# SiLU of the gates placed behind the last softmax exponential in a hybrid attention and recurrence layer

## The chip, the cores and the metric

The kernel runs on one core of one Trainium2 chip. The metric is the device time of one execution in microseconds (us), lower being better. The core has five engines with a program each: PE (TensorE, matrix products; its weight loads are listed as PEld), DVE (VectorE), ACT (ScalarE), POOL (GpSimd) and SP (SyncE, which here only starts transfers). Each engine executes its own program strictly in order; they wait for each other by semaphores. All numbers are float32, and each product is made of three passes over high and low halves (fp32r).

## The reference, cut to what matters

One encoder layer on 512 tokens of width 2048. A single input projection gives six parts:

```python
h = rms_norm(x, norm_w)
q, k, v, g_attn, xr, g_lru = split(h @ w_in)
attn_out = attention_group(q, k, v, ...)        # 8 heads of 128, 2 key/value heads, softmax over 512 keys
lru_out  = lru_group(xr, ...)                   # convolution, gated linear recurrence in both directions
mixed = concat([rms_norm(attn_out) * silu(g_attn), rms_norm(lru_out) * silu(g_lru)])
return x + mixed @ w_out
```

The part that matters here is `silu(g_lru)` and the first quarter of `silu(g_attn)`, and when they are computed relative to the softmax.

## The kernel before, in words

The layer is written as stages along PE's time. First the projection of `xr` and the recurrence, then k, v and q, then, from about 256 to 434 us of the profile, the attention. The attention's products leave PE with gaps while softmax runs elsewhere, so a second stream of work is woven into it: `fill = gates()`, a generator. The attention yields small numbers of steps, and `weave(fill, attention(rots))` takes so many steps of `gates()` between its pieces. A step `n` of `gates()` is half a letter of `PLAN`: `u` is a block of the recurrence's gate `g_lru` (`gl_units`, seven products P1, Q6, P2, Q5, Q3, Q7, Q4 of a Strassen-Winograd scheme, whose sums end in eight tiles `halves_of`, named ev in the profile), `G` a block of the first 256 columns of `g_attn` (`ga_units`, two tiles `early`), `H` a block of the next 256 columns (`late`).

Beside each step a side generator `todo` may take a step: the gating. `lru_gates(j)` handles four ev tiles, tokens by features: SiLU with the scale `rstd` (L1228), a second scaling by `r_lru` (L1231), and four groups of four transposes on PE (L1236) into one PSUM bank each, from which DVE multiplies into `hp`, the recurrence's output (L1240). `heads_gates` applies SiLU to the two `early` tiles (L1248) and multiplies into the first heads on DVE (L1252). In the kernel before, `lru_gates(0)` and `heads_gates` are started when the last `G` is done and `lru_gates(1)` when Q4 is done.

Softmax is in `softmax`: the row maximum on DVE (L626), its scaling on ACT (L627), the exponential on ACT (L630), a reciprocal on DVE and the division on POOL (L632). It is done 32 times (8 heads, 4 blocks of queries). The weights are transposed on PE (L639) and split on ACT and DVE (L581, L582). `values` multiplies them with v and copies the result on ACT (L652).

ACT also makes the high half of each weight tile (`wsplit`, L224, tiles wr to wh; for `ga_units` L1211) and of the second operand of the scheme (draw to dh, L1183); DVE makes the low halves (wl, L226 and L1212; dl, L1184). wr has three buffers, and wh and wl four each.

What orders an engine's program: PE, POOL and (in this stage) the transfers follow the order of the code; for ACT and DVE a scheduler chooses by priorities and by when inputs are ready. `tc.issue_after(ins)` adds an order on one engine: what is recorded inside stands behind `ins` in that engine's program. It adds no semaphore.

Exponential and SiLU need different function tables on ACT. Between them stands an instruction ACT_TABLE_LOAD, put there by the compiler wherever the function changes from one table to the other; copies and Identity need no change.

Of the kernel before, what the change touches and what calls it, by code (L numbers as in the profile page):

```python
# [13 lines left out]
AF = mybir.ActivationFunctionType  # L14
# [11 lines left out]
G = NH // NKV  # L26
# [36 lines left out]
def hybrid_kernel(  # L63
# [20 lines left out]
    nc = tc.nc  # L84
# [30 lines left out]
    def nm(s):  # L115
        cnt[0] += 1
        return f"{s}_{cnt[0]}"
# [7 lines left out]
    def k2(dt=F32, shape=(P, SEQ)):  # L125
        pool, n, _ = work()
        return pools[pool].tile(list(shape), dt, tag="k2", bufs=n, name=nm("k2"))
# [11 lines left out]
    def pj():  # L139
        return ps.tile([P, SEQ], F32, tag="pj", name=nm("pj"))  # L140

    def mm():
        return ps.tile([P, SEQ], F32, tag="mm", name=nm("mm"))

    def const(shape, name, dt=F32):
        return cp.tile(list(shape), dt, tag=name, name=name)
# [45 lines left out]
    def v1(r):  # L192
        return vec[:, r : r + 1]
# [95 lines left out]
    rstd = const([P, NT], "rstd")  # L289
# [320 lines left out]
    def weights(q, g, t, r, by):  # L610

        qh, ql = q
        tt = slice(t * P, (t + 1) * P)
        sc = mm()
        mm3(sc, qh[:, tt], ql[:, tt], kth[g], ktl[g], True, True)
        return soon(softmax, sc, r, by=by)

    def soon(what, *given, by=SOON):

        with tc.high_priority(by):  # L620
            return what(*given)

    def softmax(sc, r):

        mx = pools["att"].tile([P, 1], F32, tag="mx", bufs=16, name=nm("mx"))
        nc.vector.tensor_reduce(mx, sc, axis=AX.X, op=ALU.max, negate=True)  # L626
        nc.scalar.activation(mx, mx, AF.Identity, scale=r)  # L627
        p = k2()
        sm = pools["att"].tile([P, 1], F32, tag="sm", bufs=16, name=nm("sm"))
        nc.scalar.activation(p, sc, AF.Exp, bias=mx, scale=r, accum_out=sm)  # L630
        nc.vector.reciprocal(sm, sm)  # L631
        nc.gpsimd.tensor_scalar(p, p, sm, 0.0, op0=ALU.mult, op1=ALU.add)  # L632
        return p
# [86 lines left out]
    def group_rstd(src, name, n):  # L720

        pr = mm()
        for t in range(NT):
            for k, part in enumerate(src):
                nc.tensor.matmul(
                    pr[:, t : t + 1], part[:, t * P : (t + 1) * P], ones[:, 0:1],
                    start=k == 0, stop=k == len(src) - 1,
                )
        r = const([P, NT], name)
        nc.vector.tensor_copy(r, pr[:, :NT])  # L730
        rsqrt_mean(r, r, n, NT)
        return r
# [9 lines left out]
    P1, Q6, Q5, Q7, P2, Q3, Q4 = (0, 0), (5, 5), (4, 3), (3, 4), (2, 2), (6, 1), (1, 6)  # L742
# [425 lines left out]
    def gl_units(banks):  # L1168

        nd = 0  # L1170
        for name, left, right in PRODUCTS:
            for c in range(4):
                with tc.high_priority(AHEAD):
                    raw = pools["wr"].tile([P, 2, SEQ], F32, tag="wr", bufs=3, name=nm("wr"))
                    nc.sync.dma_start(
                        raw, gsum[c][right] if isinstance(right, int) else two_gl(c, *right)
                    )
                    if isinstance(left, int):
                        draw = draws[nd % 2]
                        nd += 1  # L1180
                        nc.sync.dma_start(draw, dsum[c][:, left])
                        dh, dl = d_tiles()
                        nc.scalar.copy(dh, draw)  # L1183
                        nc.vector.tensor_sub(dl, draw, f(dh))  # L1184
                    ws = [wsplit(raw, n) for n in range(2)]
                for n, (wh, wl) in enumerate(ws):
                    i = 2 * c + n
                    for s, bank in enumerate(banks):
                        if isinstance(left, int):
                            lh, ll = (t[:, n, s * P : (s + 1) * P] for t in (dh, dl))  # L1190
                        else:
                            k, t = left
                            ts_ = slice(t * H + s * P, t * H + (s + 1) * P)
                            lh, ll = xh[2 * i + k][:, ts_], xl[2 * i + k][:, ts_]
                        mm3(bank, lh, ll, wh, wl, i == 0, i == KT // 2 - 1)
                    if i == KT // 2 - 1:
                        product_done(name, banks)
                    yield name if i == KT // 2 - 1 else None

    def ga_units(part, res, banks):  # L1200

        for c in range(KT // 2):
            with tc.high_priority(AHEAD):
                raw = pools["wr"].tile([P, 2, SEQ], F32, tag="wr", bufs=3, name=nm("wr"))
                src = w_in[c * 2 * P : (c + 1) * 2 * P, C_GA + part * H : C_GA + (part + 1) * H]
                nc.sync.dma_start(raw[:, :, :H], src.rearrange("(k p) e -> p k e", p=P))
                wh, wl = (
                    pools["xw"].tile([P, SEQ], F32R, tag=t, bufs=4, name=nm(t)) for t in ("wh", "wl")
                )
                wh, wl = (t.rearrange("p (k e) -> p k e", k=2) for t in (wh, wl))  # L1210
                nc.scalar.copy(wh, raw[:, :, :H])  # L1211
                nc.vector.tensor_sub(wl, raw[:, :, :H], f(wh))  # L1212
            for e, bank in enumerate(banks):
                es = slice(e * P, (e + 1) * P)
                for k in range(2):
                    kk = 2 * c + k
                    mm3(
                        bank, wh[:, k, es], wl[:, k, es], xh[kk], xl[kk], kk == 0, kk == KT - 1
                    )
                if c == KT // 2 - 1 and e == 1:  # L1220
                    res.extend(evac_bc(banks))
                yield None

    def lru_gates(j):

        tiles = [halves_of[n, s] for n in (("c", "d"), ("b", "a"))[j] for s in range(2)]
        for t, tile_ in enumerate(tiles):
            nc.scalar.activation(tile_, tile_, AF.Silu, scale=rstd[:, t : t + 1])  # L1228
        yield
        for t, tile_ in enumerate(tiles):  # L1230
            nc.scalar.activation(tile_, tile_, AF.Identity, scale=r_lru[0][:, t : t + 1])  # L1231
        yield
        for m in range(4):
            pt = mm()
            for t, tile_ in enumerate(tiles):
                nc.tensor.transpose(  # L1236
                    pt[:, t * P : (t + 1) * P], tile_[:, m * P : (m + 1) * P], ident
                )
            dst = hp[2 * j + m // 2][:, m % 2, :]
            nc.vector.scalar_tensor_tensor(  # L1240
                dst, dst, v1(R_LN + 4 * j + m), pt, op0=ALU.mult, op1=ALU.mult
            )
            yield

    def heads_gates(res):

        for g in res:
            nc.scalar.activation(g, g, AF.Silu)  # L1248
        yield
        for e, g in enumerate(res):  # L1250
            dst = ap_[0][:, e, :]
            nc.vector.scalar_tensor_tensor(  # L1252
                dst, dst, v1(R_AN + e), g, op0=ALU.mult, op1=ALU.mult
            )
            yield

    PLAN = "GGuuuuG" "uuuuG" "uuuuG" "uuuuG" "uuuuG" "uuuuG" "uuuu" "HHHHHHHH"

    def gates():
        early, b = [], [pj() for _ in range(4)]  # L1260
        units = {"u": gl_units(b[:2]), "G": ga_units(0, early, b[2:]), "H": ga_units(1, late, b[2:])}
        todo = iter(())
        for n, unit in enumerate(itertools.chain.from_iterable((u, u) for u in PLAN)):
            done = next(units[unit])
            if n >= 4 and n % 2 == 0:
                next(out_sums, None)
            if done == "Q4":
                todo = itertools.chain(todo, lru_gates(1))
            elif unit == "G" and len(early) == 2 and n == PLAN.rindex("G") * 2 + 1:
                todo = itertools.chain(lru_gates(0), heads_gates(early))  # L1270
            else:
                next(todo, None)
            yield

    fill = gates()
    with tc.manual_schedule(engines={mybir.EngineType.Pool}):
        weave(fill, attention(rots))
        for _ in range(8):
            next(fill)
    r = group_rstd([sums["a"]], "r_a", NH * HD)  # L1280
# [106 lines left out]
```

## Time and profile before

| quantity | value |
|---|---|
| median of 3 runs | 646.5 us (645.63 to 648.03) |
| the profiled execution | 647.2 us |
| its span, first to last instruction | 645.4 us |
| PE busy | 638.1 us (99%) |
| DVE, ACT, POOL busy | 507.8, 392.8, 135.3 us |
| granted TensorE clock | 1.000 |

The profiled execution is one of its own, 0.7 us over the median; 1.8 us of it lie outside the span. In the rows, the first number is the start in us from the span's start, the second the duration; "[1.36 <-DVE pt L582]" says that the engine sat idle 1.36 us before it and that the end of that DVE instruction released it. Tile names stand without their numbers.

### The profile page before, as it was taken

The page shows a single profiled execution, that of the slowest core. Times are in us where ns is not written, and L with a number is a line of the kernel's source. Part 1 is how long each engine was busy: PE and PEld are TensorE (multiplying, and loading weights), DVE is VectorE, ACT ScalarE, POOL GpSimd, SP SyncE. Part 2 cuts the span into 40 slices and gives each one's busy share as a digit, 9 for nine tenths or more (in the row PEclk, how much of TensorE's full clock was granted, in tenths as well). Part 3 has the DMA queues.
Part 4 walks back from the last instruction along what each step waited for, and adds up shares of the span by engine and source line. Part 5 has one row for each costly group of instructions (what it writes and reads, how often), then busy time and mean ns, then how long its engine had stood idle before and what let it go on. Part 6 is the DMA issues. An engine that isn't in the chain of part 4 may idle for free.

```text
span 645.4 us, 8955 instructions
## 1 busy us (share of the span) xinstructions
PE 638.1 (99%) x2962; PEld 528.0 (82%) x2962; DVE 507.8 (79%) x886; ACT 392.8 (61%) x733; POOL 135.3 (21%) x173
## 2 busy tenths in 40 slices
PE   9999999999999999999999989999999999999997
PEld 6887888888888888888888868788888888888886
DVE  5777679996799994977677868749928978699994
ACT  3542799579955524877697797765434654443441
POOL 0003303232250501533433243211000000010000
PEclk9999999999999999999999999999999999999999
DMA  8856976888868544499989967763354857575322
GB/s 291 273 158 178 261 205 141 252 197 203 201 176 226 172 158 168 150 251 299 232 225 268 280 167 202 162 151 113 97 191 174 313 172 241 196 281 211 119 94 98
DMA packets 68782, 128.19 MB, mean 199 GB/s; under 512 B 5504, under 2 KB 24320, under 8 KB 68480
## 3 DMA queue, kind: packets, MB, share of 16 engines
q1 hardware_dynamic: 55856, 90.25, 42.5%
q0 software_dynamic: 12704, 37.23, 25.2%
q8 instruction: 23, 0.38, 0.2%
q14 instruction: 23, 0.19, 0.1%
q10 hardware_dynamic: 176, 0.14, 0.1%
HBM read 119.21 MB, written 41.95 MB: 250 GB/s over the span
## 4 chain that ended last, share of the span: by engine, by line
PE 90%; ACT 4%; DMA 3%; DVE 1%; issue 1%; SPq 0%; ACTq 0%
PE pj L152 18%; PE pj L153 18%; PE pj L154 18%; PE mm L992 13%; PE pj L992 11%; PE mm L153 3%; PE mm L152 3%; PE mm L154 3%; PE mm L639 1%; DMA wr<-gs 1%; DMA wr<-in_w_in_dram 1%; ACT wh L224 1%; PE mm L256 1%; PE mm L577 1%; ACT k L630 1%
## 5 line engine op out<-in xcount | busy, mean ns | idle before, releaser
L224 ACT CAST wh<-wr 128x512 fp32r<-128x512 f32 x151 | 90.1, 618 | 63.5 <-PE pj L154 23.6
L226 DVE TENSOR_TENSOR wl<-wr,wh 128x512 fp32r<-128x512 f32 (+1 forms) x153 | 104.6, 705 | 29.5 <-ACT wh L224 28.2
L152 PE MATMUL pj<-x,wh 128*128 128x512 f32 x248 | 98.1, 396 | 0.0
L153 PE MATMUL pj<-x,wh 128*128 128x512 f32 x248 | 96.7, 390 | 0.4 <-DVE x L259 0.4
L154 PE MATMUL pj<-x,wl 128*128 128x512 f32 x248 | 96.7, 390 | 0.0
L152 PE MATMUL pj<-wh,x 128*128 128x512 f32 x240 | 94.1, 392 | 0.0
L154 PE MATMUL pj<-wh,x 128*128 128x512 f32 x240 | 93.5, 389 | 0.0
L153 PE MATMUL pj<-wl,x 128*128 128x512 f32 x240 | 93.4, 389 | 0.0
L786 ACT CAST oh<-rw 128x512 fp32r<-128x512 f32 x94 | 56.3, 620 | 38.8 <-PE mm L992 15.5
L787 DVE TENSOR_TENSOR ol<-rw,oh 128x512 fp32r<-128x512 f32 x94 | 61.8, 686 | 10.8 <-ACT oh L786 9.2
L152 PEld LDWEIGHTS pj<-x,wh 128*128 128x128 f32 x248 | 46.6, 188 | 10.2 <-DVE ev L413 0.3
L153 PEld LDWEIGHTS pj<-x,wh 128*128 128x128 f32 x248 | 46.6, 188 | 9.9 <-DVE x L259 0.7
L154 PEld LDWEIGHTS pj<-x,wl 128*128 128x128 f32 x248 | 46.5, 188 | 9.9
L154 PEld LDWEIGHTS pj<-wh,x 128*128 128x128 f32 x240 | 45.0, 188 | 9.4
L152 PEld LDWEIGHTS pj<-wh,x 128*128 128x128 f32 x240 | 45.1, 188 | 9.2
L153 PEld LDWEIGHTS pj<-wl,x 128*128 128x128 f32 x240 | 45.1, 188 | 9.2
L992 PE MATMUL mm<-ol,mh 128*128 128x512 f32 (+1 forms) x128 | 49.0, 382 | 0.0
L992 PE MATMUL mm<-oh,ml 128*128 128x512 f32 (+1 forms) x128 | 48.9, 382 | 0.0
L992 PE MATMUL mm<-oh,mh 128*128 128x512 f32 (+1 forms) x128 | 48.9, 382 | 0.0
L924 POOL DMA_DIRECT2D out_dram<-xt x12 | 6.5, 542 | 189.5 <-DVE xt L960 139.8
L632 POOL TENSOR_SCALAR k<-k,sm 128x512 f32<-128x512 f32 x32 | 27.5, 891 | 66.0 <-DVE sm L631 34.7
L992 PE MATMUL pj<-oh,mh 128*128 128x512 f32 (+1 forms) x104 | 39.7, 382 | 0.0
(240 smaller groups left out, 1360.8 us busy)
## 6 DMA issues: line engine op xcount, KB each, us to landing
wr<-in_w_in_dram SPq DMA_DIRECT2D x59, 512.0 KB, 4.1
rw<-in_w_out_dram SPq DMA_DIRECT2D x63, 256.0 KB, 3.8
gs<-in_w_in_dram POOLq DMA_DIRECT2D x24, 512.0 KB, 6.9
ts<-in_w_out_dram POOLq DMA_DIRECT2D x24, 512.0 KB, 7.8
wr<-gs SPq DMA_DIRECT2D x16, 512.0 KB, 5.8
rw<-ts SPq DMA_DIRECT2D x31, 256.0 KB, 4.6
wr<-in_w_in_dram SPq DMA_DIRECT2D x17, 256.0 KB, 4.5
gs<-gs POOLq DMA_DIRECT2D x8, 512.0 KB, 7.4
```

The source lines that it names most:

```text
L152: nc.tensor.matmul(acc, lh, rh, start=start, stop=False)
L153: nc.tensor.matmul(acc, lh, rl, start=False, stop=False)
L154: nc.tensor.matmul(acc, ll, rh, start=False, stop=stop)
L224: rounded(hi[:, c], raw[:, k, c])
L226: nc.vector.tensor_sub(lo[:, c], raw[:, k, c], f(hi[:, c]))
L256: nc.tensor.transpose(pt[:, t * P : (t + 1) * P], xc[:, h * n + t, ks], ident)
L577: nc.tensor.transpose(pt[:, t * P : (t + 1) * P], rot[t][:, h, :], ident)
L632: nc.gpsimd.tensor_scalar(p, p, sm, 0.0, op0=ALU.mult, op1=ALU.add)
L786: nc.scalar.copy(hi, src)
L787: nc.vector.tensor_sub(lo, src, f(hi))
L924: (queue or nc.gpsimd).dma_start(of[t * P : (t + 1) * P, os_], xts[g][t][:, cs])
L992: nc.tensor.matmul(bank[key][:, to], lh[:, a, ts_], rh[:, cols], start=i == 0 and j == 0, stop=i == 7 and j == 2,)
```

## The change

`softmax` remembers its latest exponential. Each SiLU of `lru_gates` and `heads_gates` is placed behind that exponential on ACT. The side generator is no longer started by the products' ends but at step `GATED = 70`, when all 32 exponentials have been recorded: first `lru_gates(0)`, then `lru_gates(1)`, then `heads_gates`.

```diff
+    last_exp = [None]
 ...
-        nc.scalar.activation(p, sc, AF.Exp, bias=mx, scale=r, accum_out=sm)
+        last_exp[0] = nc.scalar.activation(p, sc, AF.Exp, bias=mx, scale=r, accum_out=sm).ins
 ...
         for t, tile_ in enumerate(tiles):
-            nc.scalar.activation(tile_, tile_, AF.Silu, scale=rstd[:, t : t + 1])
+            with tc.issue_after(last_exp[0]):
+                nc.scalar.activation(tile_, tile_, AF.Silu, scale=rstd[:, t : t + 1])
 ...
         for g in res:
-            nc.scalar.activation(g, g, AF.Silu)
+            with tc.issue_after(last_exp[0]):
+                nc.scalar.activation(g, g, AF.Silu)
 ...
+    GATED = 70
 ...
-            if done == "Q4":
-                todo = itertools.chain(todo, lru_gates(1))
-            elif unit == "G" and len(early) == 2 and n == PLAN.rindex("G") * 2 + 1:
-                todo = itertools.chain(lru_gates(0), heads_gates(early))
-            else:
-                next(todo, None)
+            if n == GATED:
+                todo = itertools.chain(lru_gates(0), lru_gates(1), heads_gates(early))
+            next(todo, None)
```

Lines behind the insertions move down by two to five; the names of lines in the text are those of the kernel before. ACT's program goes from 657 to 649 rows; POOL's and SP's keep their order.

On ACT, in the second half of the attention, before (a row is a line, an operation, the tiles written and read, and the shape; numbers tell buffers of one name apart):

```order
L224 CAST wh_3980<-wr_3973 128x512
L1228 ACT_TABLE_LOAD
L1228 ACTIVATE ev_3838<-ev_3838,rstd 128x512
L581 CAST pt_3860<-mm_3862 128x4x128
L581 CAST pt_3860<-mm_3869 128x4x128
L652 COPY av_3855<-mm_3842 128x512
L1228 ACTIVATE ev_3840<-ev_3840,rstd 128x512
L657 ACTIVATE k_825_3857<-av_3855 128x512
L1231 ACTIVATE ev_3838<-ev_3838,r_l 128x512
L627 ACTIVATE mx_3880<-mx_3880,q_r_96 128x1
L1231 ACTIVATE ev_3840<-ev_3840,r_l 128x512
L630 ACT_TABLE_LOAD
```

The SiLU of two tiles stood, with a table load, between the cast of a weight tile (wh_3980) and the casts of transposed softmax weights (pt_3860), and a second table load ahead of the next exponential. The same place now:

```order
L224 CAST wh_3980<-wr_3973 128x512
L654 COPY av_3855<-mm_3842 128x512
L581 CAST pt_3860<-mm_3862 128x4x128
L581 CAST pt_3860<-mm_3869 128x4x128
L659 ACTIVATE k_825_3857<-av_3855 128x512
L629 ACTIVATE mx_3880<-mx_3880,q_r_96 128x1
L632 ACTIVATE k_832_3883,sm_3884<-mm_3876,mx_3880,q_r_96 128x512
L629 ACTIVATE mx_3905<-mx_3905,q_r_97 128x1
L632 ACTIVATE k_839_3908,sm_3909<-mm_3901,mx_3905,q_r_97 128x512
```

The two table loads, two SiLUs and two scalings are gone from here, and the copy of the values (av_3855) has come ahead of the two casts.

On ACT, after the last exponential, before (from the last table load for an exponential on):

```order
L630 ACT_TABLE_LOAD
L630 ACTIVATE k_911_4206,sm_4207<-mm_4199,mx_4203,q_r_99 128x512
L581 CAST pt_4274<-mm_4276 128x4x128
L1211 CAST wh_4384<-wr_4382 128x512
L581 CAST pt_4274<-mm_4283 128x4x128
L652 COPY av_4269<-mm_4256 128x512
L657 ACTIVATE k_922_4271<-av_4269 128x512
L1211 CAST wh_4404<-wr_4402 128x512
L581 CAST pt_4274<-mm_4324 128x4x128
L581 CAST pt_4274<-mm_4331 128x4x128
L1211 CAST wh_4430<-wr_4428 128x512
L1211 CAST wh_4460<-wr_4458 128x512
```

and now, the last part of what stands between the last exponential and the eighth SiLU or scaling of the first four tiles:

```order
L1213 CAST wh_4358<-wr_4356 128x512
L1231 ACTIVATE ev_3838<-ev_3838,rstd 128x512
L1213 CAST wh_4388<-wr_4386 128x512
L581 CAST pt_4254<-mm_4292 128x4x128
L581 CAST pt_4254<-mm_4299 128x4x128
L1231 ACTIVATE ev_3840<-ev_3840,rstd 128x512
L1234 ACTIVATE ev_3588<-ev_3588,r_l 128x512
L1213 CAST wh_4418<-wr_4416 128x512
L1234 ACTIVATE ev_3590<-ev_3590,r_l 128x512
L1213 CAST wh_4444<-wr_4442 128x512
L1234 ACTIVATE ev_3838<-ev_3838,r_l 128x512
L1234 ACTIVATE ev_3840<-ev_3840,r_l 128x512
```

The SiLUs (L1231 in the changed kernel) and scalings (L1234) of the first four tiles now stand among the casts of the `H` weights (L1213), of which wh_4444 stands ahead of the last two scalings.

On PE, at the end of the attention, before (first gating transposes of the four that stood ahead of the last transposes of weights):

```order
L152 MATMUL pj_2637<-wh_4223,x_73_305 128x512
L153 MATMUL pj_2637<-wl_4224,x_73_305 128x512
L154 MATMUL pj_2637<-wh_4223,x_74_306 128x512
L1236 MATMUL mm_4238<-ident,ev_3588 128x128
L1236 MATMUL mm_4238<-ident,ev_3590 128x128
L1236 MATMUL mm_4238<-ident,ev_3838 128x128
L1236 MATMUL mm_4238<-ident,ev_3840 128x128
L152 MATMUL pj_2636<-wh_4227,x_85_352 128x512
L153 MATMUL pj_2636<-wl_4228,x_85_352 128x512
```

and now, where the first gating transposes stand behind the last value products and one block of `H`:

```order
L154 MATMUL mm_4339<-pt_4254,v_2002 128x512
L152 MATMUL pj_2638<-x_42_181,wh_4358 128x512
L153 MATMUL pj_2638<-x_43_182,wh_4358 128x512
L154 MATMUL pj_2638<-x_42_181,wl_4359 128x512
L152 MATMUL pj_2638<-x_54_215,wh_4358 128x512
L153 MATMUL pj_2638<-x_55_216,wh_4358 128x512
L154 MATMUL pj_2638<-x_54_215,wl_4359 128x512
L1239 MATMUL mm_4368<-ident,ev_3588 128x128
L1239 MATMUL mm_4368<-ident,ev_3590 128x128
L1239 MATMUL mm_4368<-ident,ev_3838 128x128
L1239 MATMUL mm_4368<-ident,ev_3840 128x128
```

Four of the eight groups of gating transposes have moved from ahead of the last value products to behind them; all eight now stand among the blocks of `H`.

## Prediction

> **What bounds the kernel now.** I read the page's busy times and the chain that ended last first, then stretches of the attention, then PE's own rows there, then what ACT did ahead of each gap.
>
> ```profile
> PE 638.1 (99%) x2962; PEld 528.0 (82%) x2962; DVE 507.8 (79%) x886; ACT 392.8 (61%) x733; POOL 135.3 (21%) x173
> PE 90%; ACT 4%; DMA 3%; DVE 1%; issue 1%; SPq 0%; ACTq 0%
> 255.00:340.00 85.00, 85.00 (x417) 70.97 (x416) 64.39 (x117) 69.21 (x159) 36.58 (x45) 1.00 0.80 225
> 340.00:372.00 32.00, 32.00 (x163) 26.87 (x162) 25.79 (x43) 23.27 (x48) 10.70 (x14) 1.00 0.93 273
> ```
>
> PE is the bound: 99% of the span, and 90% of the chain. A change elsewhere is worth only what PE waits. In the attention's first 117 us (the two stretches: length, then PE's busy time) PE never waits. All that can be won lies in a few gaps after 372 us. These are the rows around each:
>
> ```profile
> 371.85 0.39 PE L153 MATMUL pj<-x,wh 128*128 128x512 f32 x1
> 372.07 0.39 PE L154 MATMUL pj<-x,wl 128*128 128x512 f32 x1
> 373.82 0.50 PE L152 MATMUL mm<-kt,b 128*128 128x512 f32 x1 [1.36 <-DVE pt L582]
> 374.16 0.39 PE L153 MATMUL mm<-kt,b 128*128 128x512 f32 x1
> ...
> 381.43 0.39 PE L154 MATMUL pj<-wh,dl 128*128 128x512 f32 x1
> 382.30 0.50 PE L152 MATMUL mm<-kt,b 128*128 128x512 f32 x1 [0.49 <-ACT k L630]
> 382.64 0.40 PE L153 MATMUL mm<-kt,b 128*128 128x512 f32 x1
> ...
> 403.71 0.39 PE L154 MATMUL pj<-wh,x 128*128 128x512 f32 x1
> 403.95 0.60 PE L1236 MATMUL mm<-ident,ev 128*128 128x128 f32 x4
> 404.30 0.48 PE L152 MATMUL pj<-wh,x 128*128 128x512 f32 x1
> 404.61 0.40 PE L153 MATMUL pj<-wl,x 128*128 128x512 f32 x1
> ...
> 410.99 0.39 PE L154 MATMUL pj<-wh,x 128*128 128x512 f32 x1
> 411.56 0.66 PE L1236 MATMUL mm<-ident,ev 128*128 128x128 f32 x4 [0.18 <-ACT k L630]
> 411.97 0.48 PE L152 MATMUL pj<-wh,x 128*128 128x512 f32 x1
> ...
> 413.44 0.60 PE L1236 MATMUL mm<-ident,ev 128*128 128x128 f32 x4
> 413.88 1.04 PE L639 MATMUL mm<-ident,k 128*128 128x128 f32 x8
> ...
> 417.53 0.39 PE L152 MATMUL mm<-pt,v 128*128 128x512 f32 x1
> 418.03 0.50 PE L153 MATMUL mm<-pt,v 128*128 128x512 f32 x1
> 418.37 0.39 PE L154 MATMUL mm<-pt,v 128*128 128x512 f32 x1
> ...
> 420.67 0.39 PE L152 MATMUL pj<-x,wh 128*128 128x512 f32 x1
> ```
>
> Matmuls overlap, so the loss is read from the starts: undisturbed, one starts every 0.23 us (371.85 to 372.07), a group of four transposes takes 0.35 (403.95 to 404.30), and the matmul behind it takes 0.31 instead of 0.23. I measure each gap up to the second start behind it, because the first matmul after a wait is slow too.
>
> - First: 372.07 to 374.16 is 2.09, undisturbed 0.46: 1.63 lost.
> - Second: 381.43 to 382.64 is 1.21, less 0.46: 0.75.
> - Third: 410.99 to 411.97 is 0.98, against 0.59 at 403.71 to 404.30: 0.39.
> - Fourth: 413.44 to 413.88 is 0.44, less 0.35: 0.09.
> - Fifth: 417.53 to 418.37 is 0.84, less 0.46: 0.38.
>
> Together 3.24 us, 0.5% of the time. That is also about what a measurement here tells from no change.
>
> **Whose fault the gaps are.** ACT's rows ahead of them, with one row of DVE, and first a row of the chain:
>
> ```profile
> 360.85 8.99 DMA wr<-gs
> ...
> 369.92 0.62 ACT L224 CAST wh<-wr 128x512 fp32r<-128x512 f32 x1 [0.79 <-DMA wr<-gs]
> 370.55 1.28 ACT L1228 ACT_TABLE_LOAD   x1
> 371.85 0.72 ACT L1228 ACTIVATE ev<-ev,rstd 128x512 f32<-128x512 f32 x1
> 372.48 1.05 ACT L581 CAST pt<-mm 128x512 fp32r<-128x512 f32 x2
> 373.42 0.60 ACT L652 COPY av<-mm 128x512 f32<-128x512 f32 x1
> 373.07 1.29 DVE L582 TENSOR_TENSOR pt<-mm,pt 128x512 fp32r<-128x512 f32 x2 [1.74 <-ACT pt L581]
> 376.58 1.28 ACT L630 ACT_TABLE_LOAD   x1
> ...
> 381.38 0.78 ACT L630 ACTIVATE k<-mm,mx,q_r 128x512 f32<-128x512 f32 x1
> ...
> 407.39 1.28 ACT L1248 ACT_TABLE_LOAD   x1
> ...
> 409.34 1.28 ACT L630 ACT_TABLE_LOAD   x1
> 410.64 0.78 ACT L630 ACTIVATE k<-mm,mx,q_r 128x512 f32<-128x512 f32 x1
> ```
>
> ACT has just waited for a late weight load (9.0 us under way); then a table load and a SiLU, 1.93 us from 370.55 to 372.48, go ahead of the two casts pt that free PE's bank. The second gap ends with an exponential (381.38) held up in the queue behind the next table load at 376.58, the third with the one (410.64) behind 409.34; the fourth and fifth are the tail of the same queue (casts and their low halves on DVE). So all five stand behind SiLU and its table loads.
>
> **The change part by part.**
>
> *Table loads.* Seven in the attention's second half become one. Six times 1.28 is 7.7 us off ACT. Off PE's path is only what the gaps hold, because elsewhere ACT's lateness is covered by PE's other blocks.
>
> *First gap.* Now after the cast at 369.92 follow the copy av and the two casts. A cast took at most 0.63 (369.92 to 370.55), a read from PSUM 0.47 (two in 372.48 to 373.42). So av, for whose bank PE now waits, is read by 369.92 + 0.63 + 0.47 = 371.0, while PE arrives at 372.07 + 0.23 = 372.3. The gap closes with 1.3 us to spare: -1.63, or nothing if the load lands over 1.3 us later.
>
> *Second and third gap.* Exponentials without table loads ahead: the one of 381.38 comes forward by the load at 376.58, a SiLU and the first gap (over 3 us, and the gap it makes is 0.75), that of 410.64 by two loads and a SiLU: -0.75 and -0.39; 0 at the other end, if another wait stands right behind. The fourth, -0.09, held the transposes that move.
>
> *Fifth gap.* The last casts pt stood behind that queue; now one table load and three SiLUs stand ahead of them (1.30 + 3 x 0.63 = 3.2 us), where before there were two loads and a SiLU (3.2). But now everything before is earlier by the first two gaps and the transposes moved from here. I take it as closed (-0.38), with 0 as the other end.
>
> *Gating transposes.* The same 32 on PE. Before, the fourth group ran straight into L639's; now it stands alone, one slow matmul more: 0.31 - 0.23 = +0.08. The products on DVE that read them are the same.
>
> *New wait at the first gating transposes.* On PE they now stand one block of six matmuls behind the last value products: 420.67, less 3.24 of gaps and four moved groups (4 x 0.43), is 415.7, plus 6 x 0.23 is 417.1. They need ACT's fourth scaling. ACT's queue: the last cast of a `u` weight waits (four buffers) until PE is through with the block that began at 404.30; six matmuls on, less the first two gaps (2.38) and one moved group (0.43), that is 403.0; the cast ends at about 403.7. From there to the fourth scaling stand one table load (1.30), eight SiLUs and scalings (5.04), four casts (2.52), five reads of PSUM (2.35) and a square (at most 0.63): 11.8 us, so 415.5. That is 1.6 us before PE: 0.
>
> *But one of these casts, wh_4444, waits for a transfer.* Its buffer is free when DVE has made the low half after the cast wh_4358: 403.7 + 1.30 + 0.63 + 1.41 + 0.63 + 0.63 + 0.63 = 408.9, plus DVE's 0.7: started at 409.7. The same load before:
>
> ```profile
> 412.52 1.04 POOL L838 DMA_DIRECT2D ts<-in_w_out_dram  x1
> 413.33 0.37 SPq L1206 DMA_DIRECT2D wr<-in_w_in_dram  x1
> 419.61 0.62 ACT L1211 CAST wh<-wr 128x512 fp32r<-128x512 f32 x1 [2.65 <-DMA wr<-in_w_in_dram]
> DMA to landing us min/median/max: 2.8/4.5/6.0
> ```
>
> It was started just behind a 512 KB transfer of POOL, and ACT had it 6.3 us later; loads of this stretch take 2.8 to 6.0, median 4.5. POOL's next transfer will again start about half a us ahead of it (the square, then 1.3 us of addition). With 6.3 it is there at 416.0, the cast and two scalings (1.89) end at 417.9: PE waits 0.8. With 4.5 it waits 0. I take 0.4.
>
> *Sum.* 647.2 (the profiled execution) - 3.24 + 0.08 + 0.4 = 644.4. The median is 0.7 lower. If those 0.7 are the same waits turned out smaller, the sum stays; if they lie elsewhere, it is 643.7. I forecast 644.2.
>
> The Trainium skill, "ScalarE: Activation LUTs", section What ACT_TABLE_LOAD costs, gives 1283 ns for the load, which the rows agree with, and a drain of about 1380 ns on top, 2.66 us for each switch. The rows here show no such drain: SiLU starts 1.30 after the load's start. By the page the one load left would put ACT's queue 1.4 us later, the wait at the first gating transposes at up to 2.2 and the sum at about 645.8.
>
> **The rivals.**
>
> *The wait moves (slower).* The load of wh_4444 lands so late that the first gating transposes give everything back. It decides at 3.16 us of wait: landing at 418.4, 8.7 us after its start. For it: a load took 8.99 in the rows above. Against: none of its own stretch took over 6.3. At 9.0 it lands at 418.7, ACT is done at 420.6, PE waits 3.5: 647.5. Chance 0.12. The skill's "Trainium Kernel Development and Optimization", Key Constraints, says that all queues share the same 16 DMA engines; the slow load behind POOL's transfer agrees.
>
> *The first gap belongs to the transfer, not to the table.* Its load lands over 1.3 us later than here, or the fifth gap stays: 644.2 + 1.6 to 2.0, about 646. For it: 9 us under way is long and can vary. Against: the slack above. Chance 0.14.
>
> *ACT was the true bound.* In this stretch it is busy almost throughout; each load gone is 1.28 off PE: 647.2 - 7.7 = 639.5. Against: PE's whole loss there is 3.24. Chance 0.05.
>
> *The change does nothing*, because SiLU and exponential still alternate: the program has one table load there, so below 0.02, at 646.5.
>
> **How the numbers follow.** Forecast 0.67, rivals 0.12, 0.14, 0.05, 0.02. The forecast's own range is 643.2 (median scale, no new wait, all gaps) to 645.3 (0.8 of wait, fifth gap kept). The range 643.0 to 646.9 leaves out the true-bound rival, most of the slower one and the ends of the scatter. Faster by over 0.5% is below 643.3: a fifth of the forecast's share and the 0.05, together 0.18. Slower by over 0.5% is above 649.7: a load slower than any in the trace, 0.04. Within: 0.78.
>
> **What would show it.** One table load between 300 us and 434 us; PE's rows unbroken at the first three gaps; ACT's wait for the load ahead of the fourth L1211 cast, and whether PE idles before the first gating transposes. I am wrong if PE shows an idle time over 1 us between 372 and 420 or new ones in the 210 us behind, where it has none to give back now.

## The result and the profile after

The changed kernel takes 642.97 us (median of 5 runs, 642.56 to 643.48), the kernel before, run beside it, 646.61 (645.63 to 648.03): ratio 0.9943, 95% interval 0.9928 to 0.9958. Forecast was 644.2 with a range from 643.0. The change gains 3.6 us where 2.3 were forecast, 0.6% instead of 0.4%.

The page of after, busy times and engines of the chain (compare PE 638.1, ACT 392.8 and PE 90%, ACT 4%, DMA 3%):

```profile
PE 635.7 (99%) x2962; PEld 528.0 (82%) x2962; DVE 510.6 (80%) x886; ACT 382.3 (60%) x725; POOL 133.1 (21%) x173
PE 97%; DMA 1%; SPq 0%; DVE 0%; ACT 0%; issue 0%
```

Eight instructions fewer on ACT, all table loads (8 x 1.28 = 10.3 of the 10.5 us less; the prediction counted six, from the second half of the attention alone), and ACT is gone from the chain. All waits of PE in after, with the sum, the times and the longest:

```profile
PE mm L1033 <- DVE ones L159: 1.0, 1, 1.0
PE pj L153 <- DVE x L259: 0.4, 1, 0.4
```

Both are in the first 14 us. PE waits for nothing in the rest of the 640.8. PE's rows where the first, fourth and fifth gap stood, and at the first gating transposes, on the scale of after, which is 1.38 us ahead of before's at 369 us:

```profile
370.69 0.39 PE L154 MATMUL pj<-x,wl 128*128 128x512 f32 x1
370.92 0.39 PE L152 MATMUL mm<-kt,b 128*128 128x512 f32 x1
...
407.58 0.39 PE L154 MATMUL pj<-wh,x 128*128 128x512 f32 x1
407.82 1.03 PE L641 MATMUL mm<-ident,k 128*128 128x128 f32 x8
...
411.43 0.39 PE L152 MATMUL mm<-pt,v 128*128 128x512 f32 x1
411.65 0.39 PE L153 MATMUL mm<-pt,v 128*128 128x512 f32 x1
...
415.28 0.39 PE L154 MATMUL pj<-x,wl 128*128 128x512 f32 x1
415.51 0.60 PE L1239 MATMUL mm<-ident,ev 128*128 128x128 f32 x4
415.86 0.48 PE L152 MATMUL pj<-x,wh 128*128 128x512 f32 x1
```

Every start is 0.22 to 0.24 behind the last, and the group of four at 415.51 takes its undisturbed 0.35. ACT's rows around the first gap and ahead of the first gating transposes:

```profile
369.19 0.62 ACT L224 CAST wh<-wr 128x512 fp32r<-128x512 f32 x1 [1.71 <-DMA wr<-gs]
369.71 0.58 ACT L654 COPY av<-mm 128x512 f32<-128x512 f32 x1
370.19 1.08 ACT L581 CAST pt<-mm 128x512 fp32r<-128x512 f32 x2
...
402.83 1.28 ACT L1231 ACT_TABLE_LOAD   x1
404.12 0.72 ACT L1231 ACTIVATE ev<-ev,rstd 128x512 f32<-128x512 f32 x1
...
411.66 0.75 ACT L1234 ACTIVATE ev<-ev,r_l 128x512 f32<-128x512 f32 x1
413.68 0.62 ACT L1213 CAST wh<-wr 128x512 fp32r<-128x512 f32 x1 [1.27 <-DMA wr<-in_w_in_dram]
414.21 1.33 ACT L1234 ACTIVATE ev<-ev,r_l 128x512 f32<-128x512 f32 x2
415.45 1.32 ACT L1231 ACTIVATE ev<-ev,rstd 128x512 f32<-128x512 f32 x2
```

The copies follow the cast at 369.19 at once, as forecast. One table load is left, and SiLU starts 1.29 behind its start. The cast wh_4444 (413.68) does wait for its transfer, 1.27 us, but the last two scalings end at about 415.5, just as PE comes: no wait, and nothing to spare.

**Where the microseconds lie.** Four of PE's rows divide a run: the first L153 (near 13 us), the first L577, the first transposes of weights behind 367 us, and the first product of the output projection. Before, then after:

```profile
14.09 0.50 PE L153 MATMUL pj<-x,wh 128*128 128x512 f32 x1 [0.39 <-DVE x L259]
...
224.17 0.60 PE L577 MATMUL mm<-ident,kv 128*128 128x128 f32 x4
...
369.37 1.03 PE L639 MATMUL mm<-ident,k 128*128 128x128 f32 x8
...
488.85 0.39 PE L992 MATMUL mm<-oh,mh 128*128 128x512 f32 x1
```

```profile
13.12 0.50 PE L153 MATMUL pj<-x,wh 128*128 128x512 f32 x1 [0.38 <-DVE x L259]
...
222.79 0.60 PE L577 MATMUL mm<-ident,kv 128*128 128x128 f32 x4
...
367.99 1.03 PE L641 MATMUL mm<-ident,k 128*128 128x128 f32 x8
...
484.23 0.39 PE L994 MATMUL mm<-oh,mh 128*128 128x512 f32 x1
```

From 369.37 to 488.85 before took 119.48 us; from 367.99 to 484.23 after took 116.24. The difference, 3.24, is the sum of the five gaps to the hundredth; the repeat below agrees to 0.03, so the last digit is luck. The other 1.38 between these two executions arose before 224 us, where the change touches nothing. I call the time between the last two of these rows "the stretch"; for every run below it is given here. The ratio is to executions of before that ran beside each; their median was 646.27 beside the two repeats, order only and queue only, and 646.39 beside the last four:

| run | L577 at | stretch | time of that execution | median of its runs | ratio to before (95%) |
|---|---|---|---|---|---|
| before, as shown | 224.17 | 119.48 | 647.2 | 646.61 | |
| before, again | 223.02 | 119.86 | 646.43 | 646.43 | 0.9998 (0.9988 to 1.0008) |
| after, as shown | 222.79 | 116.24 | 642.56 | 642.97 | 0.9943 (0.9928 to 0.9958) |
| after, again | 222.97 | 116.25 | 642.76 | 643.02 | 0.9947 (0.9934 to 0.996) |
| order only | 222.86 | 120.95 | 647.76 | 647.68 | 1.0022 (1.0012 to 1.0031) |
| queue only | 223.07 | 125.81 | 652.41 | 653.16 | 1.0104 (1.0089 to 1.0119) |
| no table switch | 222.67 | 117.29 | 643.52 | 643.92 | 0.9962 (0.9948 to 0.9975) |
| one load more | 222.65 | 117.55 | 644.35 | 644.08 | 0.9961 (0.9947 to 0.9974) |
| turnings at 68 | 222.62 | 119.60 | 645.76 | 647.10 | 1.001 (0.9999 to 1.0022) |
| pairs, at 72 | 222.76 | 116.11 | 642.44 | 642.44 | 0.9938 (0.9924 to 0.9952) |

### The profile page after: what moved, and what is told of

Same layout as the page of the kernel before. It is cut to its first block, busy times and chain, and to the rows that moved or that the text cites. A ratio compares the mean times of both kernels' runs of the same rounds, so it can differ in the third digit from the quotient of the medians.

```text
span 640.8 us, 8950 instructions
## 1 busy us (share of the span) xinstructions
PE 635.7 (99%) x2962; PEld 528.0 (82%) x2962; DVE 510.6 (80%) x886; ACT 382.3 (60%) x725; POOL 133.1 (21%) x173
## 4 chain that ended last, share of the span: by engine, by line
PE 97%; DMA 1%; SPq 0%; DVE 0%; ACT 0%; issue 0%
PE pj L152 20%; PE pj L154 20%; PE pj L153 20%; PE mm L994 13%; PE pj L994 11%; PE mm L154 3%; PE mm L152 3%; PE mm L153 3%; PE mm L641 2%; DMA wr<-in_w_in_dram 1%; PE mm L256 1%; PE mm L577 1%; PE mm L1239 1%; SPq L210 0%; PE mm L727 0%; SPq L245 0%
## 5 line engine op out<-in xcount | busy, mean ns | idle before, releaser
L226 DVE TENSOR_TENSOR wl<-wr,wh 128x512 fp32r<-128x512 f32 (+1 forms) x153 | 106.5, 720 | 31.0 <-ACT wh L224 29.8
L153 PE MATMUL pj<-x,wh 128*128 128x512 f32 x248 | 96.7, 390 | 0.4 <-DVE x L259 0.4
L153 PE MATMUL pj<-wl,x 128*128 128x512 f32 x240 | 93.4, 389 | 0.0
L153 PEld LDWEIGHTS pj<-x,wh 128*128 128x128 f32 x248 | 46.6, 188 | 9.8 <-DVE x L259 0.7
L153 PEld LDWEIGHTS pj<-wl,x 128*128 128x128 f32 x240 | 45.1, 188 | 9.3
L994 PE MATMUL pj<-ol,mh 128*128 128x512 f32 (+1 forms) x104 | 39.7, 382 | 0.0
```

What stands on the lines that cost most here:

```text
L153: nc.tensor.matmul(acc, lh, rl, start=False, stop=False)
L226: nc.vector.tensor_sub(lo[:, c], raw[:, k, c], f(hi[:, c]))
L994: nc.tensor.matmul(bank[key][:, to], lh[:, a, ts_], rh[:, cols], start=i == 0 and j == 0, stop=i == 7 and j == 2,)
```

## The experiments

Theory: the gain is the five gaps and nothing else, and it takes both halves, since they are made by what stands between an exponential and the next copy on ACT. Rivals: one half carries it (the table loads, or the transposes' place), or part of it comes from elsewhere.

**Both kernels again**, unchanged.

> The kernel before once more, for the base of the sum. Theory (the 647.2 of the profiled execution stood 0.6 above the median because its first weights landed late, 7.64 against 6.26 in the execution of after, before anything that the change touches): this execution's time lies 0.5 to 1.5 us below 647.2, its first wait-released matmul between 13.1 and 14.1, and the same five gaps stand between 369 and 420, 3.2 us in sum within 0.3. Rival (the five gaps themselves vary from execution to execution): their sum differs by over 0.5 us and the start does not.

> The changed kernel once more. Theory (the five closed gaps are the whole gain, 3.24 us, less 0.08 for one more lone group of transposes): 3.2 us under the kernel before, 643.4 against 646.6, and again no wait of TensorE after the start of the program. Rival (some 0.4 us more come from elsewhere): 3.6 us under, 643.0. Second rival (the load of the fourth H weight lands only by luck before the first gating transposes): a wait of 0.1 to 0.8 us stands at 415.5 in this execution. Where the profiled start is as in the first execution of before, the first wait-released matmul stands at 14.09, where it is as in the first of after, at 13.12.

Before, the first two of the four rows, and the three gaps with an idle time in the trace, the first with the rows on both sides from which its loss is read:

```profile
13.36 0.50 PE L153 MATMUL pj<-x,wh 128*128 128x512 f32 x1 [0.23 <-DVE x L259]
...
223.02 0.60 PE L577 MATMUL mm<-ident,kv 128*128 128x128 f32 x4
...
370.93 0.39 PE L154 MATMUL pj<-x,wl 128*128 128x512 f32 x1
372.95 0.50 PE L152 MATMUL mm<-kt,b 128*128 128x512 f32 x1 [1.64 <-DVE pt L582]
373.29 0.40 PE L153 MATMUL mm<-kt,b 128*128 128x512 f32 x1
...
381.44 0.50 PE L152 MATMUL mm<-kt,b 128*128 128x512 f32 x1 [0.50 <-ACT k L630]
...
410.81 0.66 PE L1236 MATMUL mm<-ident,ev 128*128 128x128 f32 x4 [0.29 <-ACT k L630]
```

The execution that I predicted from was the odd one: L577 at 224.17, in all nine others between 222.62 and 223.07. Its first L153 was late too (14.09 against 13.36 here). So its distance to the median lay before 224 us and not in the gaps. The gaps do vary as well, but the other way. Read from the starts as in the prediction, they lose 1.90 (370.93 to 373.29, less 0.46), 0.77, 0.50, 0.08 and 0.40 here: 3.65 in sum, more than the 3.2 within 0.3 that I expected, and less than the rival asked for. The stretch is 119.86 less 116.24, 3.62, longer than in after, so that in this pair too the five gaps account for the difference. The change takes away 3.24 or 3.6 according to the execution of before.

After repeats to 0.01 in the stretch, without a wait there. Its median, 643.02, stands where the rival put it and not at 643.4; but the executions of before beside it had a median of 646.27, 3.25 higher, which is the theory's gain. The times alone do not tell the two apart.

**The order alone.**

```diff
             with tc.issue_after(last_exp[0]):      # taken out, at both places;
                 nc.scalar.activation(..., AF.Silu) # GATED = 70 and the new todo stay
```

> Only the turnings are moved; the SiLUs stay where the order of before has them on ScalarE, with all their table loads. Theory (the loads and SiLUs between the exponentials make the gaps): gaps one, two and five stay as in before (1.63, 0.75 and 0.38), and at the transposes of the last two weights TensorE, which lost the two groups of gating transposes and their products ahead of it, now waits about 2.8 us for the last exponential, where before waited 0.39 and 0.09: 648.9, 2.3 us slower than before. Rival (where the transposes stand matters, not the table loads): as fast as after, 643.0. Second rival (the half does nothing): 646.6.

Its PE rows at the first and second gap and at the last transposes of weights:

```profile
373.23 0.50 PE L152 MATMUL mm<-kt,b 128*128 128x512 f32 x1 [1.72 <-DVE pt L582]
...
381.71 0.50 PE L152 MATMUL mm<-kt,b 128*128 128x512 f32 x1 [0.45 <-ACT k L632]
...
411.14 0.63 PE L641 MATMUL mm<-ident,k 128*128 128x128 f32 x4
413.35 0.63 PE L641 MATMUL mm<-ident,k 128*128 128x128 f32 x4 [1.58 <-DVE pt L582]
```

Slower than before, by 1.1 to 1.5 us in the stretch and 0.2% in time. Gaps one and two stand where they stood, and the transposes of the last two weights now wait in full: in before, four groups of gating transposes stood ahead of them and filled that time. Expected were 2.3 us; the wait was about 1.9 instead of 2.8, and the fifth gap did not come back, though the table loads are all there. So the fifth gap hung on the order of PE's work as well.

**The queue alone.** The `todo` of before, with both `issue_after`.

> Only the SiLUs are queued behind the exponential recorded last; the turnings stand where before has them. Theory: one table load instead of seven in the stretch, gaps one and two go, but the first gating transposes now stand some 8.4 us ahead of the end of their scalings (last exponential ends at 402.2 on the time scale of after, then one load of 1.28 and eight passes of 0.63, to 408.5; TensorE is there at 400.1): 651.4, 4.9 us slower than before, with one wait of TensorE for ScalarE of 8 to 9 us at the first gating transposes. Rival (the table loads alone are the cost, the place of the transposes is free): 643 to 644.

Its one wait of PE behind the start, two windows (length, PE busy with count, ..., the granted clock third from the end) and two of PE's rows after the wait:

```profile
PE mm L1239 <- ACT ev L1234: 6.6, 1, 6.6
```

```profile
399.00:407.00 8.00, 1.56 (x7) 0.94 (x5) 3.10 (x7) 7.55 (x15) 2.74 (x5) 0.88 0.77 181
407.00:420.00 13.00, 12.48 (x58) 9.74 (x59) 6.29 (x10) 9.36 (x17) 2.98 (x3) 0.81 0.34 61
```

```profile
410.08 0.63 PE L154 MATMUL pj<-wh,x 128*128 128x512 f32 x1
410.50 0.63 PE L152 MATMUL pj<-wh,x 128*128 128x512 f32 x1
```

Gaps one and two are gone, and the place does matter: the stretch is 9.57 us longer than in after, 8.4 expected. The wait and the transposes that follow it are 8.3 of it; the remaining 1.2 is lost by the matmuls behind them, which start 0.42 apart instead of 0.23. The granted clock shows why: it falls from 1.00 to 0.50 at about 405.1 us, 4.7 after the pause began at 400.4, and is back at 411.9, about 5 us behind the end of the pause. The median of the times is 6.9 above before's (646.27), 4.9 expected. The Trainium skill, "TensorE: Matmul & The Clock Gate", Part 1: The HAM clock gate, says that TensorE's clock falls to half after an idle window of about 3.4 us; these rows agree.

So each half alone makes the kernel slower, and together they make it faster: the queue takes the loads out from between the exponentials, and the order gives ACT the time that the queue costs.

**No table switch, everything else in before's place.**

```diff
-nc.scalar.activation(tile_, tile_, AF.Silu, scale=rstd[:, t : t + 1])
+nc.scalar.activation(tile_, tile_, AF.Square, scale=rstd[:, t : t + 1])
-nc.scalar.activation(g, g, AF.Silu)
+nc.scalar.activation(g, g, AF.Square)
```

> The kernel before with a square in place of the ten SiLUs of these gates (it leaves the SiLU out), so that the passes stay between the exponentials and the table loads among them go. Theory: what makes the gaps is all that stands between an exponential and the next copy, loads and passes alike. Gap one stays at 1.6 to 2.1, since three passes of 0.63 now stand ahead of the copies of the transposed weights where one load of 1.28 and one pass stood; gaps two to five (1.61 in sum), which had two to four loads ahead of them, go: 644.6 to 645.1. Rival (the table loads are the whole cost): 643.0 to 643.3, with no gap over 0.3 us. Second rival (the loads are hidden, the passes' place is the cost): 646.3, all five gaps.

ACT's rows ahead of the first gap, and PE's row behind it, the only one of the five left:

```profile
369.30 1.33 ACT L1228 ACTIVATE ev<-ev,rstd 128x512 f32<-128x512 f32 x2
370.54 0.71 ACT L1231 ACTIVATE ev<-ev,r_l 128x512 f32<-128x512 f32 x1
371.15 0.56 ACT L652 COPY av<-mm 128x512 f32<-128x512 f32 x1
```

```profile
371.77 0.50 PE L152 MATMUL mm<-kt,b 128*128 128x512 f32 x1 [0.81 <-ACT av L652]
```

The stretch is 1.05 longer than in after and 2.2 to 2.6 shorter than in before: with the passes left in place, taking away the table loads brings some two thirds of the gain; what is left is one gap, with three passes of ACT ahead of the copy that frees PE's bank. I expected 1.6 to 2.1 for that gap. It came to 1.05, since the order of ACT also changed: the copy of av now went ahead of the casts, and PE could take av's bank. (How much that alone brings was not separated.)

**The price of the slack.** The fourth SiLU becomes an exponential.

```diff
-nc.scalar.activation(tile_, tile_, AF.Silu, scale=...)
+nc.scalar.activation(tile_, tile_, AF.Exp if (j, t) == (0, 3) else AF.Silu, scale=...)
```

> The changed kernel with an exponential in place of the fourth of its ten SiLUs (it leaves that SiLU out): one table load more ahead of the scalings, one behind. It prices the slack at the first gating transposes. Theory (ScalarE ends its scalings at 415.5 just as TensorE comes, with no slack): the load and the cast of the fourth H weight, which now stands ahead of all four scalings and waits for its transfer until 413.7, put the end of the scalings at 416.8, and TensorE waits 1.3 us: 644.3. Rival (the 1.27 us that ScalarE waits for that transfer takes the load up): 643.0, no wait. Second rival (both loads count in full): 645.6.

ACT, then PE at the first gating transposes:

```profile
410.54 1.28 ACT L1231 ACT_TABLE_LOAD   x1
411.84 0.72 ACT L1231 ACTIVATE ev<-ev,rstd 128x512 f32<-128x512 f32 x1
...
414.42 0.62 ACT L1213 CAST wh<-wr 128x512 fp32r<-128x512 f32 x1 [1.35 <-DMA wr<-in_w_in_dram]
414.95 2.56 ACT L1234 ACTIVATE ev<-ev,r_l 128x512 f32<-128x512 f32 x4
```

```profile
416.95 0.33 PE L1239 MATMUL mm<-ident,ev 128*128 128x128 f32 x1 [0.28 <-ACT ev L1234]
417.56 0.33 PE L1239 MATMUL mm<-ident,ev 128*128 128x128 f32 x1 [0.29 <-ACT ev L1234]
```

1.31 more in the stretch, 1.3 expected, and the time 1.1 above after: there is no slack. This is not the extra load's own length (1.28) showing. ACT still idles 1.35 us for the transfer ahead of the cast at 414.42, as it idled 1.27 in after; what costs is that two scalings which stood ahead of that cast in after (2 x 0.62) now stand behind it, as the theory had it. What a load alone would cost with ACT's order kept was not measured. Less than half of the loss shows as idle time (0.57): the third and the fourth transpose wait each for its own scaling and start slowly behind it, so that the loss must be read from the starts.

**The turnings two steps earlier**, `GATED = 68`.

> The changed kernel with the turnings two steps earlier, between the last transposes of weights and the value products. TensorE comes to the first gating transposes at 410.05 on the time scale of after (407.82, and 0.87 for the transposes, 6 products of 0.227), and ScalarE ends the scalings at about 413.5 (fourth SiLU to 410.54, one cast of 0.52, four passes of 0.62). Theory: one wait of 3.4 us there, 646.4, all of the gain gone. Rival (there is slack, the place within the last products is free): 643.0. Second rival (a pause of this length also lowers the granted clock behind it, as the one of 6.6 us did): 647.5 to 648.5.

The profiled execution has 3.36 more in the stretch, 3.4 expected, in four waits:

```profile
PE mm L1239 <- ACT ev L1234: 2.5, 4, 1.1
```

The median is higher by another 1.3 than this execution's 645.76, and the mean granted clocks of the ten executions go with it: three at 1.0 take 645.76 to 646.32, five at 0.997 and two at 0.995 take 646.87 to 648.73. The theory's wait is there, and the second rival's lower clock and time fit the seven slower executions; only this one has a trace, so their waits are not known.

**Pairs of groups, two steps later.**

```diff
-            yield
+            if m % 2:
+                yield
-    GATED = 70
+    GATED = 72
```

> The changed kernel with the gating transposes in four pairs of groups instead of eight single groups, and two steps later, where ScalarE has 2.7 us more. Theory (a lone group costs 0.47 us, 415.51 to 417.34 less six products of 0.227; a pair 0.87, from the transposes of weights): 4 x 0.07 = 0.3 us less between 369 and 484 us of the trace than in after (116.24), 642.7, which the times can't tell from 643.0. Rival (the pairs wait for their accumulators, since two are taken at once): 643.3 or more, with waits of TensorE for VectorE at the second groups.

No wait, and the stretch is 116.11, 0.13 less than in after; the rival's wait for accumulators didn't come. 642.44 is the best median of all, but its interval overlaps that of after: 0.13 us is all that the trace supports. What it does bring is slack. PE reaches the first pair at 418.23 and the scalings end at about 415.8, so that by these two times a transfer up to 2.4 us late would no longer cost time; that is an estimate, not a run.

## Why the prediction missed

The mechanism held: all five gaps lay behind SiLU and its table loads (the fifth hung on the order of PE's work too), all five closed, nothing was lost behind them, and their sum as measured from the starts is the stretch's difference in both executions of before (3.24 and 3.24; 3.65 and 3.62). What failed are terms of the sum around it: the base, put at 647.2 where the median was 646.5 to 646.6, and a new wait of 0.4, where none came. Each is small, and all go in one direction.

- *The base.* I summed against the profiled execution (647.2) and kept most of its 0.7 above the median, in case it lay in the same waits. It lay before 224 us. The sum on the median's scale, 643.7, was there in the text and was the right one: 0.5 of the error. One row of the trace bears on it, the first weights' load, under way for 7.64 us (6.26 in after); but only the comparison with a second execution shows it.
- *The new wait at the first gating transposes.* 0.4 taken between 0 and 0.8; 0.0 came, in both executions of after. PE came at 415.51 where 417.1 less 1.38 = 415.7 was worked out, and the transfer of wh_4444 was started at 409.4 (409.7 less 1.38 is 408.3, so 1.1 later than worked out), but it landed after 4.2 us and not 4.5 to 6.3. POOL's transfer, which I had put half a us ahead of it, was 3 us ahead. So the forecast of no wait at 4.5 us held, but the scalings ended just as PE came, in both executions: that the wait was 0.0 and not a few tenths was luck.
- *The lone group*, +0.08: the stretch shows nothing of it, and four lone groups fewer saved 0.13 in the run with pairs, about 0.03 each.
- *The gaps themselves* were on the small side in the one execution that I had: 3.6 in the second. This may be the last 0.3 or so, or it may be the scatter of the medians: before's was 646.61 beside after, from five executions, and 646.27 from the 23 beside the repeat. The record does not separate the two.
- *The range.* The measured median lies 0.03 below its low end, that of the repeat 0.02 above it. With the base settled, 643.7 less 0.4 and less the spread of the gaps gives 643.0 and below; the low end stood at the value that should have been the middle. The chance for over 0.5% faster was too small for the same reason.

Of the rivals, the moved wait came to nothing, though with no time to spare. The first gap did not belong to the transfer: in after the cast starts at 369.19 + 1.38 = 370.57 on before's scale, 0.65 later than before's 369.92 and within the 1.3 to spare, and the gap still closed. ACT as the true bound is out, with 10.5 us less on it and 3.2 to 3.6 in time. The Trainium skill, "ScalarE: Activation LUTs", section What ACT_TABLE_LOAD costs, gives each switch a drain of about 1380 ns on top of the load, by which the sum was 645.8. No drain is to be seen here: SiLU started 1.29 behind the start of the load in after (402.83 to 404.12), and the activation behind the extra load of the run with one load more 1.30 behind its start (410.54 to 411.84).

## What to carry to other kernels

When the bound engine idles only in a few places, sum those gaps from its starts; that sum is the gain if all close, and it belongs on the median, with the profiled execution's own offset located first (compare early rows that the change cannot touch). Queueing work behind a barrier on one engine and moving its consumers on another are one change: in this kernel either half alone was slower than neither. A gain that ends with the two engines arriving together is only as safe as the next late transfer, so place the consumer a step later where the bound engine has other work.

## What was unexpected of the hardware

Pauses of TensorE far shorter than 6.6 us may cost clock as well, in some executions and not in others. Of 49 executions of before, whose longest pause is 1.4 to 1.6 us in the two traces, seven had a mean granted clock of 0.996 or 0.997; their median is 647.4, that of the other 42 (0.999 or 1.0) is 646.3. Of the 16 executions of after, after again and the pairs, which pause nowhere behind the start, none was under 0.999. With four waits within 4 us (turnings at 68) it was seven of ten. The length of the longest pause does not explain this: it is 1.1 us there, and 1.7 in the order-only run, where only one of 12 executions was under 0.999. The runs without table switch and with one load more (pauses up to 0.8 us) had none in nine. Short pauses close together fit these counts better than single ones, but that the pauses are the cause is only inferred; where in a run the clock fell was seen only in the queue-only trace. The Trainium skill, "TensorE: Matmul & The Clock Gate", Part 1: The HAM clock gate, names a free-running window of about 3.4 us, which would let one and the same pause count in some executions only. But that section asks for an idle window, and none of these pauses is as long; no run here settles that.
